# Norms of the first block: sums of squares spread by a matrix of ones, and the reciprocal root taken on full rows

## Chip, cores, metric

The kernel runs on one core of a Trainium2 chip. The metric is the device time of one execution in microseconds; lower is better. Engines are named as the profile names them: PE (TensorE), PEld (its weight loads), DVE (VectorE), ACT (ScalarE), POOL (GpSimd), SP (SyncE, which issues most DMAs here).

## The reference, cut to what matters

A first block of two transformer layers works on two streams of 256 tokens by 1024 features, `x` and `ctx`; a second block of two more layers works on `x` alone. The change touches the modulated norms of the first block, other than the very first:

```python
def _rms_norm(x, g):
    y = xf * lax.rsqrt(jnp.mean(xf * xf, axis=-1, keepdims=True) + EPS)
    return y * g
def _modulate(x, g, shift, scale):
    return _rms_norm(x, g) * (1 + scale) + shift
...
for i in range(DEPTH):
    ax = _modulate(hx, norm1_g[i], sx1, cx1)
    ac = _modulate(hc, norm1_g[i], sc1, cc1)
    ...mixer...
    hx = hx + gx1 * yx
    hx = hx + gx2 * _mlp(_modulate(hx, norm2_g[i], sx2, cx2), mlp_w1[i], mlp_w2[i])
    if with_ctx:
        hc = hc + gc1 * yc
        hc = hc + gc2 * _mlp(_modulate(hc, norm2_g[i], sc2, cc2), mlp_w1[i], mlp_w2[i])
```

## The kernel before

**Layout.** Activations are feature-major: `hx` and `hc` are eight tiles each of 128 features by 256 tokens. A weight product is made in three passes (L322 to L324): every fp32 matrix is split into a high part and a remainder (`whi`, `wlo`; `ahi`, `alo`), and PE multiplies high by high, high by low and low by high. ACT makes the high parts (L198 for weights, L369 for activations), DVE the remainders (L201, L370).

**A norm** needs, for each token, a sum over features, that is over partitions and over eight tiles. `sq_stats` squares the tiles on ACT (L736), POOL adds the first five squares into `sqa` (L741, L743), and PE multiplies the four remaining tiles, as stationary operand, by a column of ones (L748). The result is a column: one number a token, tokens in the 128 partitions, two columns for 256 tokens. `rsqrt` turns it into 1/root: DVE multiplies and adds (L330), POOL raises to the power -0.5 (L332), both on 128 partitions x 2 columns. The modulation wants that number in every partition along a row of 256 tokens, so `bcast_cols` has PE spread the columns (L725: a column repeated 128 times as moving operand's stationary, times the identity). Then, for each of the eight tiles, DVE scales by it (L757), ACT adds the shift and makes `ahi`, DVE makes `alo`.

**Five calls** of `norm` take this way. I number them in order of time:
- N1 and N2 (L1112): before the MLP of layer 0, for `hx`, then for `hc`. The residuals of `hx` (L837) come from products of the output projection; those of `hc` follow.
- N3 and N4 (L1119): before layer 1, at the end of the MLP of layer 0, again `hx`, then `hc`.
- N5 (L1399): before the MLP of layer 1, `hx` alone.

After N1, PE works on the 96 products of `hc`'s residuals, then on 96 products that need only N1 (`order="x"`), and then on products that need N2. After N3 it is 96 products for `hc`, then 96 for queries of `hx`, then keys that need both streams (512 columns wide). After N5 every product needs N5.

**Order.** Each engine executes its instructions in the order in which they stand. That order is made when the program is built, by a scheduler that works from estimated costs, not from measured ones. `Weave` interleaves attention and products by due times written in the code. Weights are fetched and split a few tiles ahead (`Weights.get`). The other norms (the first one, those of the second block) have code of their own and stay.

Of the kernel before, what the change touches and what calls it, by code (L numbers as in the profile page):

```python
# [9 lines left out]
F32 = mybir.dt.float32  # L10
F32R = mybir.dt.float32r
I32 = mybir.dt.int32
AF = mybir.ActivationFunctionType
OP = mybir.AluOpType
# [3 lines left out]
D = 1024  # L18
# [204 lines left out]
def cols(c, n=128):  # L223
    return slice(n * c, n * c + n)
# [48 lines left out]
class Net:  # L273
# [275 lines left out]
    def start(self, first):  # L549
# [76 lines left out]
        with self.tc.manual_schedule(engines={mybir.EngineType.PE}):  # L626
# [18 lines left out]
            for op in ("a00 t b a01 l m0 f0 f1 a10 a11 m1 a20 a21 m2 f2 f3 "  # L645
                       "a30 a31 m3 f4 f5 f6 f7").split():
                o, i = op[0], op[1:]
                if o == "a":
                    part(int(i[0]), int(i[1]), cell)
                elif o == "m":  # L650
                    modulate(int(i), cell["gt"])
                elif o == "f":
                    prods(int(i))
                elif o == "t":
                    for k in range(4, 8):
                        turn(1, k)
                elif o == "b":
                    nc.scalar.copy(rb, self.bcast_cols(rstd, 4, "mm"))
                elif o == "l":
                    load("a30 a31")  # L660
# [68 lines left out]
    def sq_stats(self, tiles):  # L729
# [19 lines left out]
                                 skip_group_check=True)  # L749
        return p  # L750

    def modulate(self, h, rb, gs, sh, his, los, tok):

        nc = self.nc
        for k in range(8):
            t = self.e([128, 256])
            nc.vector.scalar_tensor_tensor(t, h[k], gs[:, k:k + 1], rb, op0=OP.mult, op1=OP.mult)  # L757
            op = self.split(his[k][:, tok], los[k][:, tok], t, sh[:, k:k + 1])
            if k == 1 and tok.start == 0:
                self.W.hold = op.ins  # L760
            if k == 1 and tok.start == 0:
                self.W.ahold = self.hi_op.ins

    def norm(self, l, which, r, h, a, ss=None):

        if ss is None:
            ss = self.sq_stats(h)
        rstd = self.rsqrt(ss, 2, 1.0 / D, 1e-6, True)
        rb = self.bcast_cols(rstd, 2)
        gs, sh = self.norm_scale(l, which)  # L770
        self.modulate(h, rb, gs[:, :, r], sh[:, :, r], a[0], a[1], cols(r, 256))

# [999 lines left out]
```

## Time and profile before

| | |
|---|---|
| Median of 3 runs | 1458.98 us (1456.5 to 1461.35) |
| Profiled execution: its own time | 1455.87 us |
| Profiled execution: span | 1454.1 us |
| PE busy | 1387.4 us, 95% of the span |
| DVE, ACT, POOL busy | 72%, 44%, 20% |
| Mean granted clock of PE | 0.979 of full speed |

The profile is of one execution; the runs differ from each other by 0.3%. "Busy" counts the time in which an engine executes, the chain is the sequence of work and waits that ended last.

### The profile page before, as it was taken

What the parts mean: (1) busy time and instruction counts of PE and PEld (TensorE: products, weight loads), DVE (VectorE), ACT (ScalarE), POOL (GpSimd) and SP (SyncE); (2) the same over time, 40 slices, a digit from 0 to 9 for tenths busy, and PEclk for the clock granted to TensorE, in tenths of its full rate; (3) what the DMA queues carried; (4) which work ended last, traced back from release to release, by engine and by line L of the source; (5) the groups of instructions that cost most, each with busy time, mean ns of one, the idle gap of its engine ahead of it and who ended that gap; (6) DMA issues with size and microseconds to landing.
All of it is one profiled execution on the core that took longest, in us unless ns stands there. A gap on an engine that the chain in (4) does not pass through costs nothing.

```text
span 1454.1 us, 24709 instructions
## 1 busy us (share of the span) xinstructions
PE 1387.4 (95%) x9585; PEld 1205.9 (83%) x9585; DVE 1049.6 (72%) x1958; ACT 642.8 (44%) x1229; POOL 294.1 (20%) x281
## 2 busy tenths in 40 slices
PE   6899999999999999999999999999899998799997
PEld 4676668988778777898989989999798788698787
DVE  4587666648977788788677766666696667886756
ACT  4355435442233222245556454544454552455552
POOL 0210010231011110151000021111302347602423
PEclk9999999999999999999999989999899999999999
DMA  9826461136577897753222155655356454454452
GB/s 315 284 73 210 141 208 41 59 110 206 168 238 269 274 304 257 270 165 100 73 88 87 59 170 178 189 188 173 111 168 194 131 185 139 131 136 149 139 157 73
DMA packets 198116, 240.32 MB, mean 165 GB/s; under 512 B 21071, under 2 KB 178544, under 8 KB 198000
## 3 DMA queue, kind: packets, MB, share of 16 engines
q1 hardware_dynamic: 188912, 234.85, 50.4%
q10 hardware_dynamic: 8576, 3.89, 1.0%
q8 instruction: 75, 1.23, 0.3%
q14 instruction: 41, 0.34, 0.1%
q0 software_dynamic: 512, 0.02, 0.0%
HBM read 236.70 MB, written 2.02 MB: 164 GB/s over the span
## 4 chain that ended last, share of the span: by engine, by line
PE 77%; DVE 10%; DMA 5%; POOL 3%; issue 2%; ACT 2%; SPq 0%; DVEq 0%; ACTq 0%; POOLq 0%
PE mm L322 21%; PE mm L323 21%; PE mm L324 21%; DMA adaw<-in_ada_w 3%; DVE wlo L201 2%; PE om L1082 2%; PE pt L1066 1%; PE s L1473 1%; PE om L1490 1%; PE mm L502 1%; PE om L1333 1%; PE s L1014 1%; PE pt L1484 1%; DMA rpbs<-rpb 1%; DVE ks L1255 1%
## 5 line engine op out<-in xcount | busy, mean ns | idle before, releaser
L201 DVE TENSOR_TENSOR wlo<-raw,whi 128x1024 fp32r<-128x1024 f32 (+3 forms) x278 | 358.8, 1299 | 135.0 <-ACT whi L198 124.5
L198 ACT CAST whi<-raw 128x1024 fp32r<-128x1024 f32 (+3 forms) x282 | 288.9, 1033 | 333.6 <-PE mm L323 246.6
L322 PE MATMUL mm<-ahi,whi 128*128 128x256 f32 (+2 forms) x1232 | 397.4, 323 | 2.5 <-ACT ahi L369 2.3
L323 PE MATMUL mm<-alo,whi 128*128 128x256 f32 (+1 forms) x1232 | 394.5, 321 | 3.4 <-DVE alo L370 3.3
L324 PE MATMUL mm<-ahi,wlo 128*128 128x256 f32 (+1 forms) x1232 | 393.4, 320 | 0.0
L322 PEld LDWEIGHTS mm<-ahi,whi 128*128 128x128 f32 (+1 forms) x1232 | 236.8, 192 | 23.9 <-issue 3.2
L323 PEld LDWEIGHTS mm<-alo,whi 128*128 128x128 f32 x1232 | 236.5, 192 | 21.5 <-DVE alo L370 4.2
L324 PEld LDWEIGHTS mm<-ahi,wlo 128*128 128x128 f32 x1232 | 236.0, 192 | 18.4 <-issue 2.4
L322 PE MATMUL mm<-hid,whi 128*128 128x256 f32 (+1 forms) x544 | 179.2, 329 | 0.0
L323 PE MATMUL mm<-hid,whi 128*128 128x256 f32 (+1 forms) x544 | 178.4, 328 | 0.0
L324 PE MATMUL mm<-hid,wlo 128*128 128x256 f32 (+1 forms) x544 | 178.0, 327 | 0.0
L368 POOL TENSOR_TENSOR hid<-e,hid 128x512 fp32r<-128x512 f32 x48 | 78.3, 1632 | 416.8 <-ACT hid L367 416.8
L534 DVE SCALAR_TENSOR_TENSOR acc<-adaw,cst,acc 128x1024 f32<-128x1024 f32 x98 | 125.2, 1292 | 1.3 <-DMA adaw<-in_w_ada 1.0
L322 PEld LDWEIGHTS mm<-hid,whi 128*128 128x128 f32 x544 | 102.8, 189 | 10.6 <-ACT whi L198 0.4
L324 PEld LDWEIGHTS mm<-hid,wlo 128*128 128x128 f32 x544 | 102.8, 189 | 10.0
L323 PEld LDWEIGHTS mm<-hid,whi 128*128 128x128 f32 x544 | 102.9, 189 | 9.4
L837 DVE SCALAR_TENSOR_TENSOR hx<-mm,cst,hx 128x256 f32<-128x256 f32 x160 | 72.4, 479 | 31.7 <-PE mm L324 31.4
L322 PE MATMUL mm<-whi,ahi 128*128 128x256 f32 (+1 forms) x192 | 57.3, 299 | 0.7 <-ACT ahi L1689 0.7
L324 PE MATMUL mm<-whi,alo 128*128 128x256 f32 (+1 forms) x192 | 56.0, 292 | 1.4 <-DVE alo L1690 1.4
L1136 ACT ACTIVATE e<-mm 128x512 f32<-128x512 f32 x48 | 28.6, 596 | 63.7 <-PE mm L324 63.5
L1138 DVE SCALAR_TENSOR_TENSOR e<-mm,e 128x512 f32<-128x512 f32 x48 | 33.0, 687 | 32.9 <-ACT e L1136 32.9
L323 PE MATMUL mm<-wlo,ahi 128*128 128x256 f32 (+1 forms) x192 | 55.7, 290 | 0.0
(319 smaller groups left out, 2389.3 us busy)
## 6 DMA issues: line engine op xcount, KB each, us to landing
raw<-in_mlp_w SPq DMA_DIRECT2D x128, 512.0 KB, 4.9
adaw<-in_ada_w SPq DMA_DIRECT2D x96, 512.0 KB, 5.1
raw<-in_w_in SPq DMA_DIRECT2D x64, 512.0 KB, 3.9
adaw<-in_w_ada SPq DMA_DIRECT2D x48, 512.0 KB, 5.5
raw<-in_odd_w_in SPq DMA_DIRECT2D x24, 512.0 KB, 3.5
raw<-in_w_out SPq DMA_DIRECT2D x16, 512.0 KB, 5.1
raw<-in_even_w_in SPq DMA_DIRECT2D x12, 512.0 KB, 6.0
raw<-in_even_w_out SPq DMA_DIRECT2D x8, 512.0 KB, 3.5
```

What stands on the lines that cost most here:

```text
L198: self.nc.scalar.copy(hi[:, :m], raw)
L201: (self.nc.gpsimd if on_pool else self.nc.vector).tensor_tensor(lo[:, :m], raw, hi[:, :m].bitcast(F32), op=OP.subtract)
L322: mm(ps, w[0], x[0], start=start, stop=False, skip_group_check=skip)
L323: mm(ps, w[0], x[1], start=False, stop=False, skip_group_check=skip)
L324: mm(ps, w[1], x[0], start=False, stop=stop, skip_group_check=skip)
L368: return (lo_eng or nc.vector).tensor_tensor(lo, t, hf, op=OP.subtract)
L502: nc.tensor.matmul(ps[32 * j:32 * j + 32], self.cs1[:, k, :], raw[:, 256 * j:256 * j + 256], start=k == 0, stop=k == 7)
L534: V.scalar_tensor_tensor(acc, raw, s, acc, op0=OP.mult, op1=OP.add)
L837: self.nc.vector.scalar_tensor_tensor(h[m], ps, self.adaT[l][:, base + m, r:r + 1], h[m], op0=OP.mult, op1=OP.add)
L1082: nc.tensor.matmul(o[64 * hh:64 * hh + 64, cols(q)], self.v[ab][:, 4 - nkt + i, cols(j // 2, 64)], PTs[q][:, i, hh], start=i == 0, stop=i ...
L1136: nc.scalar.activation(r, ps, AF.Relu)
L1138: V.scalar_tensor_tensor(t, ps, 0.0, r, op0=OP.max, op1=OP.mult)
```

## The change

`norm` no longer calls `sq_stats`, `rsqrt` and `bcast_cols`; a new function `inv_rms` takes their place. The squares and POOL's sums are as before. PE now multiplies a 128x128 matrix of ones (one column, repeated) as stationary operand by the four tiles of squares as moving operand, 256 columns each: the sum lands in all 128 partitions as a row. DVE multiplies and adds on 128 partitions x 256 columns, and POOL raises 128x256 to the power -0.5. The modulation reads that tile from SBUF.

```diff
+    def inv_rms(self, tiles):
+        nc = self.nc
+        p = self.psum("om", [128, 256])
...
+        sqs.insert(0, acc)
+        for i, sq in enumerate(sqs):
+            nc.tensor.matmul(p, self.ones.to_broadcast([128, 128]), sq, start=i == 0, stop=i == len(sqs) - 1)
+        rb = self.e([128, 256])
+        nc.vector.tensor_scalar(rb, p, 1.0 / D, 1e-6, op0=OP.mult, op1=OP.add)
+        nc.gpsimd.tensor_tensor(rb, rb, self.mhalf[:, 0:1].to_broadcast([128, 256]), op=OP.pow)
+        return rb
...
-    def norm(self, l, which, r, h, a, ss=None):
-        if ss is None:
-            ss = self.sq_stats(h)
-        rstd = self.rsqrt(ss, 2, 1.0 / D, 1e-6, True)
-        rb = self.bcast_cols(rstd, 2)
+    def norm(self, l, which, r, h, a):
+        rb = self.inv_rms(h)
         gs, sh = self.norm_scale(l, which)
         self.modulate(h, rb, gs[:, :, r], sh[:, :, r], a[0], a[1], cols(r, 256))
```

Two places show how it moves instructions. Line numbers behind the new function are higher by 20 (L837 becomes L857, L757 becomes L780).

PE at N1, in the middle of the products for `hc` (`mm<-y`): before,

```order
L748 MATMUL om<-cst,e 128x1 x2
L322 MATMUL mm<-y,whi 128x256
L323 MATMUL mm<-y,whi 128x256
L324 MATMUL mm<-y,wlo 128x256
L322 MATMUL mm<-y,whi 128x256
L748 MATMUL om<-cst,e 128x1 x2
L748 MATMUL om<-cst,sqa 128x1 x2
L323 MATMUL mm<-y,whi 128x256
L324 MATMUL mm<-y,wlo 128x256
L322 MATMUL mm<-y,whi 128x256
L323 MATMUL mm<-y,whi 128x256
L725 MATMUL om<-cst,sm 128x128 x2
```

and now:

```order
L324 MATMUL mm<-y,wlo 128x256
L769 MATMUL om<-sqa,cst 128x256
L769 MATMUL om<-e,cst 128x256
L322 MATMUL mm<-y,whi 128x256
L323 MATMUL mm<-y,whi 128x256
L769 MATMUL om<-e,cst 128x256 x2
L324 MATMUL mm<-y,wlo 128x256
```

The eight small products and the two that spread have become four of 256 columns; behind them stand 94 products of `hc` and then the first that needs N1. At N3 there are 92.

DVE between N1 and N2: before, from the first residual of `hc` to the affine step of N2 (L330),

```order
L837 SCALAR_TENSOR_TENSOR hc_135<-mm,cst,hc_135 128x256 x2
L370 SCALAR_TENSOR_TENSOR alo<-e,cst,ahi 128x256
L837 SCALAR_TENSOR_TENSOR hc_135<-mm,cst,hc_135 128x256 x2
L837 SCALAR_TENSOR_TENSOR hc_136<-mm,cst,hc_136 128x256 x4
L201 TENSOR_TENSOR wlo<-raw,whi 128x1024
L330 TENSOR_SCALAR sm<-om 128x2
```

and now, to the affine step L771:

```order
L370 SCALAR_TENSOR_TENSOR alo<-e,cst,ahi 128x256 x3
L857 SCALAR_TENSOR_TENSOR hc_135<-mm,cst,hc_135 128x256 x4
L857 SCALAR_TENSOR_TENSOR hc_136<-mm,cst,hc_136 128x256 x2
L201 TENSOR_TENSOR wlo<-raw,whi 128x1024
L857 SCALAR_TENSOR_TENSOR hc_136<-mm,cst,hc_136 128x256 x2
L201 TENSOR_TENSOR wlo<-raw,whi 128x1024 x2
L771 TENSOR_SCALAR e<-om 128x256
```

In both, the residuals of `hc` stand behind the modulation of `hx` (the L757/L780 rows ahead of these), now with one more weight split among them. At N4 the two residuals of `hc` and the split that stood ahead of the modulation have moved into it, and on POOL five DMA issues (L682) stand ahead of N3's power where three stood.

## Rows read from the trace of the kernel before

**Rows 1.** The page: the chain that ended last, share of the span by engine.

```profile
PE 77%; DVE 10%; DMA 5%; POOL 3%; issue 2%; ACT 2%; SPq 0%; DVEq 0%; ACTq 0%; POOLq 0%
```

**Rows 2.** Timeline of PE (start us, us, [idle before]): first products needing N1 to N5.

```profile
270.05 0.28 PE L322 MATMUL mm<-ahi,whi 128*128 128x256 f32 x1
...
288.36 0.28 PE L322 MATMUL mm<-ahi,whi 128*128 128x256 f32 x1
...
646.24 0.28 PE L322 MATMUL mm<-ahi,whi 128*128 128x256 f32 x1
...
661.12 0.40 PE L322 MATMUL mm<-ahi,whi 128*128 128x512 f32 x1
...
842.92 0.58 PE L322 MATMUL mm<-ahi,whi 128*128 128x256 f32 x1 [1.17 <-ACT ahi L369]
```

**Rows 3.** Line L332, the power, in four windows: ns min/median/max, first and last start.

```profile
L332 POOL TENSOR_TENSOR sm<-sm,cst x1: 1022/1022/1022, 14.0 to 14.0; 128x4 f32<-128x4 f32 x1
...
L332 POOL TENSOR_TENSOR sm<-sm,cst x1: 704/704/704, 839.8 to 839.8; 128x2 f32<-128x2 f32 x1
...
L332 POOL TENSOR_TENSOR sm<-sm,cst x1: 1613/1613/1613, 276.0 to 276.0; 128x2 f32<-128x2 f32 x1
...
L332 POOL TENSOR_TENSOR sm<-sm,cst x1: 1025/1025/1025, 1236.9 to 1236.9; 128x1 f32<-128x1 f32 x1
```

**Rows 4.** Timeline of DVE beside the last two of them.

```profile
275.85 1.22 DVE L201 TENSOR_TENSOR wlo<-raw,whi 128x1024 fp32r<-128x1024 f32 x1
...
1236.74 0.74 DVE L1676 SCALAR_TENSOR_TENSOR u<-z,sm,gsr 128x512 f32<-128x512 f32 x1
```

**Rows 5.** Timeline of POOL: the first two-input multiplication of 256 columns.

```profile
62.99 0.74 POOL L847 TENSOR_TENSOR e<-e,kc 128x256 f32<-128x256 f32 x1 [6.09 <-PE om L844]
```

**Rows 6.** Timeline of PE: an fp32 product of 256 columns (two passes) among others.

```profile
62.31 0.59 PE L844 MATMUL om<-e,kc 128*128 128x256 f32 x2
...
62.97 0.39 PE L323 MATMUL mm<-alo,whi 128*128 128x512 f32 x1
63.20 0.39 PE L324 MATMUL mm<-ahi,wlo 128*128 128x512 f32 x1
```

**Rows 7.** Timeline of DVE and ACT at N1.

```profile
255.93 0.88 DVE L837 SCALAR_TENSOR_TENSOR hx<-mm,cst,hx 128x256 f32<-128x256 f32 x2 [1.73 <-PE mm L324]
...
260.96 1.27 DVE L757 SCALAR_TENSOR_TENSOR e<-hx,sm,om 128x256 f32<-128x256 f32 x3 [1.51 <-PE om L725]
...
256.50 0.81 ACT L736 ACTIVATE e<-hx 128x256 f32<-128x256 f32 x2 [1.80 <-DVE hx L837]
...
261.48 0.51 ACT L369 ACTIVATE ahi<-e,cst 128x256 fp32r<-128x256 f32 x1 [4.17 <-DVE e L757]
```

**Rows 8.** Timeline of DVE and POOL at N2.

```profile
269.23 2.44 DVE L837 SCALAR_TENSOR_TENSOR hc<-mm,cst,hc 128x256 f32<-128x256 f32 x6
...
271.64 3.35 POOL L743 TENSOR_TENSOR sqa<-sqa,e 128x256 f32<-128x256 f32 x3 [1.26 <-ACT e L736]
```

**Rows 9.** Timeline of POOL and DVE at N3 and N4.

```profile
631.31 3.16 POOL L743 TENSOR_TENSOR sqa<-sqa,e 128x256 f32<-128x256 f32 x4 [0.74 <-ACT e L736]
634.40 1.48 POOL L682 DMA_DIRECT2D row<-adag  x3
...
639.61 1.26 DVE L757 SCALAR_TENSOR_TENSOR e<-hx,sm,om 128x256 f32<-128x256 f32 x3
...
646.55 2.05 DVE L837 SCALAR_TENSOR_TENSOR hc<-mm,cst,hc 128x256 f32<-128x256 f32 x5
```

**Rows 10.** Timeline of POOL at N5.

```profile
835.49 3.14 POOL L743 TENSOR_TENSOR sqa<-sqa,e 128x256 f32<-128x256 f32 x4
```

**Rows 11.** Window of PE at N5: us, busy (x instructions), granted clock, DMA share, GB/s.

```profile
843.00:849.00 6.00, 5.94 (x26) 0.50 0.00 0
```

**Rows 12.** Timeline of PE at N1: the last four of 16 small passes; the spreading.

```profile
258.52 0.58 PE L748 MATMUL om<-cst,sqa 128*128 128x1 f32 x4
...
260.15 0.71 PE L725 MATMUL om<-cst,sm 128*128 128x128 f32 x4 [0.47 <-POOL sm L332]
```

More of the change, by code (lines that the diff above doesn't have):

```diff
@@ L750, in sq_stats @@
         return p
+    def inv_rms(self, tiles):
+        nc = self.nc
+        p = self.psum("om", [128, 256])
+        sqs, acc = [], None
+        for i, t in enumerate(tiles):
+            sq = self.e([128, 256])
+            nc.scalar.activation(sq, t, AF.Square)
+            if i >= len(tiles) - 3:
+                sqs.append(sq)
+            elif acc is None:
+                acc = self.sb.tile([128, 256], F32, name="sqa", tag="sqa", bufs=2)
+                nc.gpsimd.tensor_copy(acc, sq)
+            else:
+                nc.gpsimd.tensor_tensor(acc, acc, sq, op=OP.add)
+        sqs.insert(0, acc)
[5 more added lines that the diff above has]
+        return rb
     def modulate(self, h, rb, gs, sh, his, los, tok):
```

## The prediction

> **What bounds the kernel now.** I read the chain that ended last first: PE holds 77% of it, DVE 10%, POOL 3% [rows 1], and the table has PE busy for 95% of the span. So a change off PE matters only where PE waits for it. I then looked on PE's timeline for the first product that needs each of the five norms: 270.05, 288.36, 646.24, 661.12 and 842.92 us [rows 2]. Only the last has PE idle in front of it (1.17 us there, for `ahi`). At N1 to N4 PE has other products to do while the norm is worked out, and it comes to the dependent product later than the norm does. At N5 there is nothing else to do. So what matters is how much later than now each norm is ready, less the slack at its landmark.
>
> **The price on which all rests: the power on POOL.** Before, it works on 2 columns; now on 256. The trace has no power of 256 columns, but it has three sizes [rows 3]. With DVE quiet, 2 columns took 704 ns and 4 columns 1022 ns: (1022 - 704)/2 = 159 ns for a column, on a base of 704 - 318 = 386 ns. The call of 4 columns is the kernel's first power; that it pays for a first use I doubt, since POOL's first two-input multiplication took 0.74 us for 256 columns [rows 5], as its later ones do.
>
> The other two sizes bear it out in a rougher way. A power that runs beside a DVE instruction with two SBUF inputs seems to stand still until that one ends. Of the call with 2 columns that began at 276.02 the DVE instruction ended at 275.85 + 1.22 = 277.07 and the power at 277.63, 0.56 later; of the call with 1 column, 1236.74 + 0.74 = 1237.48 and 1237.93, 0.45 later [rows 3, 4]. One column less is 0.11 to 0.12 us less.
>
> So 256 columns are 386 + 256 x 159 ns = 41.1 us if it goes on like this. Lower bound of this reading, by the second pair: 0.70 + 254 x 0.12 = 31 us. Upper, with some waiting for DVE: 44 us. The lowest price that any row allows is that of an ordinary multiplication of the same size, 0.74 us [rows 5]. I take 41.1, because it is the one value measured undisturbed on this very operation, and call it P.
>
> The Trainium skill ("GPSIMD Engine Reference", section 3.1) would say otherwise: a two-input elementwise instruction on POOL costs about 2.6 cycles an element at 1.2 GHz, by which the power would be an estimated 0.6 us and its start, and the sum would be a gain as in the first rival below. The trace agrees for the multiplication (0.74 us) and not for the power, whose two extra columns cost 318 ns.
>
> **The other prices.** An fp32 product of 256 columns delays PE by 0.43 us: from the start of L844's pair to that of the second product behind it are 0.66 us, of which one ordinary product is 0.23 [rows 6]. Four are 1.7 us. The affine step is one DVE instruction on 128x256, like one of the three that took 1.27 us: 0.45 with its end [rows 7]. From the first modulating instruction to its `ahi` are 261.99 - 260.96 = 1.03 us [rows 7].
>
> **Norm by norm.** Each line: when the power may start, its end, the first product, and the landmark.
> - N1. The last residual ends at 256.81, its square at 257.31 [rows 7]; the last two ones products follow (0.9) and the affine step: 258.6. Power until 299.7, product at 300.8. It stands 30.7 us behind 270.05. Slack was 10.4.
> - N2. On DVE the residuals of `hc` stand behind N1's modulation, which waits for the power; ACT's squares, POOL's sums and the ones products are queued behind those. Before, from the first modulating instruction (260.96) to the last residual of `hc` (271.67) were 10.7 us, and POOL's sum ended 3.3 later [rows 7, 8]. Now one more weight split stands among them (1.2 us, as in [rows 4]). So 299.7 + 10.7 + 1.2 + 3.3 + 1.7 + 0.45 = 317.1, power until 358.2, product at 359.2 against 288.36: 70.9 us, N1's share in it. PE's 96 products between (18.3 us before) end at about 319 and wait.
> - N3. POOL's sum ends at 634.47; five DMA issues of 0.49 stand ahead of the power [rows 9]: 636.9, by which time the ones products and the affine step are done too. Power until 678.0, product at 679.1: 32.9 us.
> - N4. First modulating instruction to last residual of `hc` were 648.60 - 639.61 = 9.0 [rows 9]; two residuals and a split have moved in (0.9 + 1.2), then 3.3, 1.7 and 0.45 as at N2: 678.0 + 16.5 = 694.5. Power until 735.6, product at 736.7 against 661.12: 75.6 us, N3's share in it. The three splits ahead of the affine step fit into the wait for POOL's sum.
> - N5. The sum ends at 838.63 [rows 10]. PE has run dry; four ones products take 1.7 us at full and 3.4 at half clock, I take 2.5. Affine step 841.6, power until 882.7, product at 883.75 against 842.92: 40.8 us.
>
> Sum: 70.9 + 75.6 + 40.8 = 187.3 us. PE's clock: at N5 now, after some 7 us of little work, the granted clock was 0.50 (1.2 of 2.4 GHz) from 843 to 849 [rows 11], which loses 3 us. N2 and N4 would have such a restart anew: + 6. At N1 and N3 it costs nothing, since PE then waits for N2 and N4.
>
> What goes on PE hides in these waits: 16 small passes (four groups of 0.5), the spreading (0.71) and the wait ahead of it (0.47) [rows 12]. That DVE reads the row from SBUF and not from PSUM, and that the tile holds one of six `e` buffers during the modulation, I take as nothing: POOL waits on nobody then, and five buffers are left. The weights of the next stage are loaded during the waits, but only as far as the ring of raw tiles reaches, so little is won back.
>
> Total: 187 + 6 = 193 us, on the profiled execution's 1455.87: **1649 us**. The median of the runs is 3 us above that execution, so the median may lie there too.
>
> **Rivals.**
> 1. *The power is as cheap as a multiplication* (0.74 us): the 4-column call was slow for a reason of its own. Then N1 to N4 stay hidden, and PE saves at each 2.0 + 0.71 + 0.47 - 1.7 = 1.5 us; N5 is ready at 841.6 + 0.74 + 1.05 = 843.4, 0.5 later than now. In all -5.5: 1450 us, faster. For it: the row of 0.74 us; against it: all three sizes of the power. This decides below about 4.4 us for the power (17 ns a column): there N5 loses 4.1 and N4, whose slack ends at 3.4, another 2.
> 2. *Long rows are interleaved*, so that a column costs a quarter of 159 ns: power 10.6 us. N1 loses nothing, N2 +9.8 (299.7 becomes 269.2, then 17.4 + 10.6 + 1.0 against 288.36), N3 and N4 together +14.5, N5 +10.3, some clock: about 1494 us. For it: rows of 1, 2 and 4 columns can't show what a loop does with 256. Against it: 2 to 4 shows no saving. The Trainium skill (same page, section 7) bears on this: a chain of dependent fp32 operations pays 4 cycles for each, and four independent chains hide that; no run here shows whether the power does so.
> 3. *The row is not needed as early*: the waits at N1 and N3 are absorbed, N2 and N4 begin early since POOL's sums don't depend on them. Then each pair costs one power: 2 x (41 - 10) + 41 + 6, about 1564. Against it: DVE's order, in which `hc`'s residuals stand behind the modulation of `hx`.
>
> **Chances and range.** The forecast 0.66 (its own range, from powers of 31 and 44 us in five places, 1599 to 1664); rival 1 0.15; rival 2, with all prices between 5 and 30 us, 0.15; rival 3 0.04. 0.3% (4 us) is about what a measurement of this kernel can tell from no change. Rival 1 gives 0.10 faster, 0.05 the same; the rest is slower: 0.85. For 8 in 10 the range takes in the forecast's own and most of rivals 2 and 3: 1485 to 1675.
>
> **What would show it.** In the changed profile L772 five times with about 41 us each, and POOL's busy time up by 200 us; PE idle before the first `mm<-ahi` at N1 (some 31 us), N2 (38), N3, N4 and N5, put down to ACT's `ahi`; the clock at half behind each. If L772 takes below 5 us, the price is wrong and rival 1 or 2 holds. If it takes 41 us and the sum is off, my queues at N2 and N4 are.

## The result and the profile after

The changed kernel takes 1667.39 us (median of 4 runs, 1664.2 to 1670.23), the kernel before 1458.36 in the same comparison: ratio 1.1434, 95% interval 1.1412 to 1.1456. The profiled execution's own time is 1664.62, its span 1662.8, 208.7 us more than before.

The page, beside [rows 1]: busy time, share of the span and instructions of two engines; PE's granted clock in tenths, in 40 slices; the chain that ended last.

```profile
PE 1399.8 (84%) x9525; PEld 1213.5 (73%) x9525; DVE 1047.1 (63%) x1958; ACT 643.4 (39%) x1229; POOL 500.4 (30%) x281
...
PEclk9999997659999999976599996899999999899999
...
PE 67%; POOL 15%; DVE 10%; DMA 4%; issue 2%; ACT 2%; SPq 0%; ACTq 0%; DVEq 0%; POOLq 0%
```

PE's busy time is nearly that of before; what was added is time in which it waits. POOL is busy 206 us more and holds 15% of the chain instead of 3%. The line of the power (ns min/median/max, first and last start), against [rows 3]:

```profile
L772 POOL TENSOR_TENSOR e<-e,cst x5: 41119/41145/41148, 256.6 to 1007.6; 128x256 f32<-128x256 f32 x5
```

What PE waited for (us in total, times, longest), its two largest waits:

```profile
PE mm L322 <- ACT ahi L369: 173.3, 6, 42.9
...
PE om L769 <- POOL sqa L766: 26.7, 5, 13.2
```

PE's timeline has the five first products of [rows 2] again, each now with its idle time in brackets, and the ones products at N2 and N4:

```profile
298.87 0.58 PE L322 MATMUL mm<-ahi,whi 128*128 128x256 f32 x1 [31.73 <-ACT ahi L369]
...
313.32 1.22 PE L769 MATMUL om<-sqa,cst 128*128 128x256 f32 x2 [13.23 <-POOL sqa L766]
...
316.69 1.68 PE L769 MATMUL om<-e,cst 128*128 128x256 f32 x4
...
361.22 0.58 PE L322 MATMUL mm<-ahi,whi 128*128 128x256 f32 x1 [32.52 <-ACT ahi L369]
...
759.08 0.58 PE L322 MATMUL mm<-ahi,whi 128*128 128x256 f32 x1 [31.99 <-ACT ahi L369]
...
773.56 1.22 PE L769 MATMUL om<-sqa,cst 128*128 128x256 f32 x2 [8.83 <-POOL sqa L766]
...
820.15 0.80 PE L322 MATMUL mm<-ahi,whi 128*128 128x512 f32 x1 [33.04 <-ACT ahi L369]
...
1049.83 0.58 PE L322 MATMUL mm<-ahi,whi 128*128 128x256 f32 x1 [42.85 <-ACT ahi L369]
```

POOL's timeline has what stands between: at N2 and N4 its last adds and the power.

```profile
306.81 6.46 POOL L766 TENSOR_TENSOR sqa<-sqa,e 128x256 f32<-128x256 f32 x4
318.99 41.12 POOL L772 TENSOR_TENSOR e<-e,cst 128x256 f32<-128x256 f32 x1 [5.72 <-DVE e L771]
...
766.74 6.77 POOL L766 TENSOR_TENSOR sqa<-sqa,e 128x256 f32<-128x256 f32 x4
777.89 41.15 POOL L772 TENSOR_TENSOR e<-e,cst 128x256 f32<-128x256 f32 x1 [4.38 <-DVE e L771]
```

Cut at the ends of the last residuals of `hx` and at the first products, the two executions compare as follows (us; the last residuals of `hx` end at 256.81, 633.05 and 837.11 before, at 254.00, 712.76 and 1002.05 now):

| stretch | before | now | more by | forecast |
|---|---|---|---|---|
| start to last residual of `hx`, layer 0 | 256.81 | 254.00 | -2.8 | 0 |
| from there to N2's product (N1, N2) | 31.55 | 107.22 | 75.7 | 70.9 |
| N2's product to the last residual ahead of N3 | 344.69 | 351.54 | 6.9 | 3 |
| from there to N4's product (N3, N4) | 28.07 | 107.39 | 79.3 | 75.6 |
| N4's product to the last residual ahead of N5 | 175.99 | 181.90 | 5.9 | 3 |
| from there to N5's product | 5.81 | 47.78 | 42.0 | 40.8 |
| N5's product to the end | 611.18 | 612.97 | 1.8 | 0 |
| sum | | | 208.7 | 193 |

The first and the last stretch hold no changed norm. In the runs below they differ from before by up to 3.7 us either way, so a difference of that size between two single executions says little.

### The profile page after: what moved, and what is told of

Its sections match the earlier page's. It is cut to its first block, busy times and chain, and to the rows that moved or that the text cites. A ratio compares the mean times of both kernels' runs of the same rounds, so it can differ in the third digit from the quotient of the medians.

```text
span 1662.8 us, 24577 instructions
## 1 busy us (share of the span) xinstructions
PE 1399.8 (84%) x9525; PEld 1213.5 (73%) x9525; DVE 1047.1 (63%) x1958; ACT 643.4 (39%) x1229; POOL 500.4 (30%) x281
## 4 chain that ended last, share of the span: by engine, by line
PE 67%; POOL 15%; DVE 10%; DMA 4%; issue 2%; ACT 2%; SPq 0%; ACTq 0%; DVEq 0%; POOLq 0%
PE mm L322 18%; PE mm L323 18%; PE mm L324 18%; POOL e L772 12%; DVE wlo L201 2%; PE om L1102 2%; DMA adaw<-in_ada_w 2%; PE pt L1086 1%; PE s L1493 1%; POOL sqa L766 1%; PE om L1510 1%; PE om L769 1%; PE mm L502 1%; DVE alo L370 1%; PE om L1353 1%
## 5 line engine op out<-in xcount | busy, mean ns | idle before, releaser
L322 PE MATMUL mm<-ahi,whi 128*128 128x256 f32 (+2 forms) x1232 | 403.3, 328 | 176.6 <-ACT ahi L369 173.3
L323 PE MATMUL mm<-alo,whi 128*128 128x256 f32 (+1 forms) x1232 | 400.5, 325 | 3.6 <-DVE alo L370 3.3
L324 PE MATMUL mm<-ahi,wlo 128*128 128x256 f32 (+1 forms) x1232 | 398.6, 324 | 0.0
L322 PEld LDWEIGHTS mm<-ahi,whi 128*128 128x128 f32 (+1 forms) x1232 | 241.4, 196 | 200.5 <-ACT ahi L369 175.1
L324 PEld LDWEIGHTS mm<-ahi,wlo 128*128 128x128 f32 x1232 | 240.7, 196 | 18.8 <-issue 2.4
L772 POOL TENSOR_TENSOR e<-e,cst 128x256 f32<-128x256 f32 x5 | 205.7, 41136 | 17.3 <-DVE e L771 17.3
L369 ACT ACTIVATE ahi<-e,cst 128x256 fp32r<-128x256 f32 x64 | 28.6, 500 | 250.0 <-DVE e L780 238.9
L857 DVE SCALAR_TENSOR_TENSOR hx<-mm,cst,hx 128x256 f32<-128x256 f32 x160 | 72.2, 477 | 32.5 <-PE mm L324 32.2
L780 DVE SCALAR_TENSOR_TENSOR e<-hx,sm,e 128x256 f32<-128x256 f32 x24 | 10.3, 479 | 123.8 <-POOL e L772 123.8
L867 POOL TENSOR_TENSOR e<-e,kc 128x256 f32<-128x256 f32 x21 | 16.8, 800 | 143.6 <-PE om L864 143.6
L780 DVE SCALAR_TENSOR_TENSOR e<-hc,sm,e 128x256 f32<-128x256 f32 x16 | 6.8, 478 | 82.5 <-POOL e L772 82.5
```

What stands on the lines that cost most here:

```text
L322: mm(ps, w[0], x[0], start=start, stop=False, skip_group_check=skip)
L323: mm(ps, w[0], x[1], start=False, stop=False, skip_group_check=skip)
L324: mm(ps, w[1], x[0], start=False, stop=stop, skip_group_check=skip)
L369: self.hi_op = nc.scalar.activation(hi, t, AF.Identity, bias=sh)
L772: nc.gpsimd.tensor_tensor(rb, rb, self.mhalf[:, 0:1].to_broadcast([128, 256]), op=OP.pow)
L857: self.nc.vector.scalar_tensor_tensor(h[m], ps, self.adaT[l][:, base + m, r:r + 1], h[m], op0=OP.mult, op1=OP.add)
```

## The experiments

My theory: the power costs 41 us because it goes column by column, and each of the loss's terms is a power that stands on a path with no cover. Rivals: another part of the row form (the affine step, the wide ones products, their order on PE) costs it; or a norm's slack is met only once in a pair, so that losses don't add up.

**e1: the power becomes a multiplication** (the root is left out).

```diff
-        nc.gpsimd.tensor_tensor(rb, rb, self.mhalf[:, 0:1].to_broadcast([128, 256]), op=OP.pow)
+        nc.gpsimd.tensor_tensor(rb, rb, self.mhalf[:, 0:1].to_broadcast([128, 256]), op=OP.mult)
```

> The changed kernel with a multiplication in place of the power on POOL, same tiles and order, so the norms' values are wrong. My theory: the whole loss is the power's price for 256 columns. Then the instruction takes 0.74 us, PE's waits for ahi at the five norms are gone but for about 1 us at the last, and the time is about 1450 us (1446 to 1456). Rival: the new form itself (ones products that stand between products on PE, an affine step behind weight splits on DVE) holds a good part of the loss; then it stays above 1470 us.

Measured: 1462.06 us, ratio to the kernel before 1.0023 [1.0013, 1.0033]. The loss of 209 us is gone, so the power is its cause. The gain of 5.5 us that my first rival gave for this case isn't there, and the time lies above the 1446 to 1456 that I expected. The line of the multiplication:

```profile
L772 POOL TENSOR_TENSOR e<-e,cst x5: 610/615/615, 258.3 to 845.6; 128x256 f32<-128x256 f32 x5
```

What PE waited for most:

```profile
PE om L769 <- POOL sqa L766: 13.0, 5, 5.4
```

And PE's timeline at N2:

```profile
274.45 1.22 PE L769 MATMUL om<-sqa,cst 128*128 128x256 f32 x2 [5.43 <-POOL sqa L766]
```

The change puts the product with POOL's sum ahead of the three others (`sqs.insert(0, acc)`); before, it came last. PE takes its instructions in order and stops there for 13.0 us in all.

**e2: powers of five sizes**, one at each norm; the rest of the tile goes without a root.

```diff
-        nc.gpsimd.tensor_tensor(rb, rb, self.mhalf[:, 0:1].to_broadcast([128, 256]), op=OP.pow)
+        np_, n = {1: (128, 128), 2: (128, 32), 3: (32, 256), 4: (128, 8), 5: (128, 64)}[self.nth]
+        nc.gpsimd.tensor_tensor(rb[:np_, :n], rb[:np_, :n], half[:np_].to_broadcast([np_, n]), op=OP.pow)
```

> The changed kernel with the power on a part of the row alone, another part at each norm (N1 128 columns in 128 partitions, N2 32 in 128, N3 256 in 32 partitions, N4 8 in 128, N5 64 in 128), the rest left without it, so values are wrong. My theory, 0.386 us and 159 ns for a column however many partitions: 20.7, 5.5, 41.1, 1.7 and 10.6 us. Rival, a price by elements: N3 at a quarter, about 10.5 us. Second rival, a loop that needs many columns to get up to speed or pays by blocks: N2, N4 and N5 off that line by more than 10%.

The groups of that line (busy us, mean ns):

```profile
L775 POOL TENSOR_TENSOR e<-e,cst 32x256 f32<-32x256 f32 x1 | 41.2, 41155 | 0.3 <-DVE e L771 0.3
...
L775 POOL TENSOR_TENSOR e<-e,cst 128x128 f32<-128x128 f32 x1 | 20.7, 20747 | 2.9 <-DVE e L771 2.9
...
L775 POOL TENSOR_TENSOR e<-e,cst 128x64 f32<-128x64 f32 x1 | 10.5, 10530 | 2.7 <-DVE e L771 2.7
...
L775 POOL TENSOR_TENSOR e<-e,cst 128x32 f32<-128x32 f32 x1 | 6.3, 6328 | 5.0 <-DVE e L771 5.0
```

The fifth, 128x8, took 1669 ns. The line 386 ns + 159 ns a column, drawn from 2 and 4 columns, gives 20.74, 10.56 and 1.66 us for 128, 64 and 8 columns. A quarter of the partitions saves nothing (32x256: 41.16). Only the 32 columns take more (5.47 by the line), which alone would speak for the second rival; but DVE began a weight split 0.16 us ahead of that power, and none ran beside the four others:

```profile
298.86 1.22 DVE L201 TENSOR_TENSOR wlo<-raw,whi 128x1024 fp32r<-128x1024 f32 x1
```

The power began at 299.02, so 1.06 us of the split ran beside it, and it took 0.85 us more than the line. The whole kernel took 1537.82 us, in a single run.

**e3 and e4: the root without POOL's power**, as a bit trick with three Newton steps on DVE (e3: 11 DVE instructions in place of the affine step and the power), or as one instruction on ACT that takes scale and bias too (e4).

```diff
-        nc.vector.tensor_scalar(rb, p, 1.0 / D, 1e-6, op0=OP.mult, op1=OP.add)
-        nc.gpsimd.tensor_tensor(rb, rb, self.mhalf[:, 0:1].to_broadcast([128, 256]), op=OP.pow)
+        nc.scalar.activation(rb, p, AF.Abs_reciprocal_sqrt, scale=1.0 / D, bias=1e-6)
```

> The changed kernel with the affine step and the power replaced by an initial guess from the bits and three Newton steps on DVE (11 instructions of 128x256, some 0.4 us each, 4.6 us a norm); values right. My theory: with no power on POOL, N1 to N4 are hidden again, N5 is ready 4.6 - 0.42 - 0.74 = 3.4 us later than in the multiplication's run: about 1454 us (1448 to 1462). Rival (the form itself costs): above 1470 us. If DVE's 4 x 4.6 us at N1 to N4 are not hidden: up to 1475.

> The changed kernel with the affine step and the power replaced by one instruction on ACT (the reciprocal root of the absolute value, scale 1/1024 and bias 1e-6 within it), which reads the sum from PSUM. My theory: about 0.5 us and two loads of ACT's tables a norm, hidden at N1 to N4; 1447 to 1460 us. Rival (the form itself costs): above 1470 us.

Measured: e3 1473.53 us, ratio 1.0102 [1.0086, 1.0119]; e4 1464.63, 1.0044 [1.0027, 1.006]. In both PE again waits 13.3 and 13.6 us at the product of POOL's sum; in e3 another 11.3 for `ahi`. Both times lie above what I expected (1448 to 1462 and 1447 to 1460): I had counted only the root's own price, as in e1.

**e5 and e6: POOL's sum last**, in e1 (e5) and in e4 (e6).

```diff
-        sqs.insert(0, acc)
+        sqs.append(acc)
```

> The multiplication's run again (values wrong), with POOL's sum as the last of the four ones products in place of the first. In that run PE stood 13.0 us before the ones products, waiting for POOL's sum; my theory is that this in-order wait ate the 5.5 us that I had forecast for a cheap power. Then the wait falls by about 1.3 us at each norm (three products of 0.43 us are done meanwhile) and more at N2, whose ones products now stand 10 products further back: 4 to 9 us less than the multiplication's 1462, that is 1453 to 1458. Rival: the wait is covered by the same products anyway, or the difference of 4 us is of another origin (the start of the program); then 1460 to 1463.

> The run with ACT's reciprocal root, with POOL's sum as the last of the four ones products; values right. My theory: the same 4 to 9 us off its 1464.6, so 1456 to 1461, the same as before the change. Rival: no difference, 1463 to 1466. Faster than 1453 neither expects.

Measured: e5 1452.45 us against 1456.12, ratio 0.9973 [0.9962, 0.9985], 9.6 us below e1 (7.9 if each is taken against the kernel before beside it); so the place of one product costs that. Cut as in the table above, e1 takes 5.6 us more than before in the five stretches from the last residual ahead of N1 to N5's product, e5 0.7 less; that e5's profile is also 3.7 us shorter behind N5's product, where nothing was changed, isn't the work of the norms. e6 1454.31, 0.9991 [0.9978, 1.0004]: no difference from the kernel before, and 10.3 us below e4 (8.6 taken as above). What PE still waits for at the ones products in e5:

```profile
PE om L769 <- ACT e L759: 5.6, 5, 2.7
```

and in e6:

```profile
PE om L769 <- ACT e L759: 6.6, 3, 2.9
```

**e7 and e8: the change for `hx` alone** (N1, N3, N5), and **for `hc` alone** (N2, N4); the other norms as before.

```diff
-        rb = self.inv_rms(h)
+        if r == 0:
+            rb = self.inv_rms(h)
+        else:
+            rb = self.bcast_cols(self.rsqrt(self.sq_stats(h), 2, 1.0 / D, 1e-6, True), 2)
```

> The change at N1, N3 and N5 (hx) alone, N2 and N4 as before; values right. My theory, one power of 41.1 us on the chain of each, N1 and N3 less their slack of some 10 us, N5 in full, restarts of PE's clock besides: about 31 + 33 + 42 + 6 on 1458, 1565 us (1555 to 1580). Rival, a price that goes by the number of powers: three fifths of 209 us, 1583.

> The change at N2 and N4 (hc) alone, the other three as before; values right. My theory: N2 about 31 us past its landmark, N4 34, two restarts of 3: 1458 + 71, 1529 us (1518 to 1538). With the run for hx the two losses then add up to some 25 us less than the whole change's 209, since each pair has slack to use once. Rival, each power for itself: two fifths of 209 us, 1541, and the two add up.

Measured, in a single run each: 1589.48 and 1542.2 us, 133.4 and 86.1 above the 1456.12 of before. Together that is 219.5, not 25 less than the whole change but more (7.5 of the 11 us more lie ahead of N1 and behind N5's product). My times of 1565 and 1529 fall; the rival's, 1583 and 1541, came closer. PE in e7, the first products of N1, N3 and N5 and what it meets behind the first two, with N2's product:

```profile
301.10 0.58 PE L322 MATMUL mm<-ahi,whi 128*128 128x256 f32 x1 [31.74 <-ACT ahi L369]
...
310.49 1.01 PE L748 MATMUL om<-cst,e 128*128 128x1 f32 x4 [7.95 <-ACT e L736]
...
328.84 0.29 PE L322 MATMUL mm<-ahi,whi 128*128 128x256 f32 x1
...
723.37 0.58 PE L322 MATMUL mm<-ahi,whi 128*128 128x256 f32 x1 [30.95 <-ACT ahi L369]
...
733.65 1.01 PE L748 MATMUL om<-cst,e 128*128 128x1 f32 x4 [5.53 <-ACT e L736]
...
974.46 0.58 PE L322 MATMUL mm<-ahi,whi 128*128 128x256 f32 x1 [42.86 <-ACT ahi L369]
```

and in e8, those of N2 and N4:

```profile
325.12 0.58 PE L322 MATMUL mm<-ahi,whi 128*128 128x256 f32 x1 [34.04 <-ACT ahi L369]
...
738.17 0.79 PE L322 MATMUL mm<-ahi,whi 128*128 128x512 f32 x1 [33.88 <-ACT ahi L369]
```

Between the last residual ahead of N1 and the one ahead of N3 lie 376.24 us before, 419.02 in e7 (255.36 + 0.88 to 672.43 + 2.83), 415.82 in e8 (257.31 + 0.88 to 671.18 + 2.83) and 458.76 in the change: +42.8 and +39.6 make 82.4, of 82.5. In the second pair, up to N5's residual, +47.2 and +41.3, of 85.2. In e7, N1's product is 31.6 us late, as forecast (30.7 at N1); then PE does a few products and stands 7.95 us more, in order, at the squares of `hc`, whose residuals waited on DVE behind N1's modulation. The other 3 us or so go at half clock. In e8 the product is 35.4 us late and 4.2 follow.

That the totals add up doesn't make each power a loss for itself. N1's lateness does reach N2, as I had it: in e7, where N2 is as before, N2's product comes 72.60 us after the last residual of `hx` (328.84 - 256.24), 41.05 later than before. With e8's 35.4 that is 76.4, where the whole change has 75.7 (46.9 and 36.1, of 79.3, in the second pair). What I had wrong is that e7 would keep the slack. N1's product is late by the power less its slack, but on the way from there to N2's product PE, stopped at the squares and at half clock, takes 27.7 us where it took 18.3, and the slack is used up. So a pair's slack comes off about once, in e8 as in the whole change.

**e9: the whole change, POOL's sum last.** The edit is that of e5, with the power.

> The whole change with its power on POOL, but the product with POOL's sum stands last among the four ones products, not first. PE no longer stops at it while three other products and, at N2 and N4, the products of hx wait behind it (26.7 us of waits in the change). My theory, each power for itself: those waits only move, since PE then does the products of hx earlier and stands longer in front of the product that needs N2; won are the parts of 5.7 and 4.4 us between the sum's end and the power's start that are more than 2, so 1661 +- 2 us. Rival: the waits at the sum add to the powers, and without them the time falls by most of 26.7 us: 1642 us.

Measured, in a single run: 1653.38 us, 11.2 below the changed kernel's profiled execution and some 8 below my 1661. What PE waited for:

```profile
PE mm L322 <- ACT ahi L369: 175.9, 6, 42.8
...
PE om L769 <- ACT e L759: 13.8, 4, 6.3
```

So of the 26.7 us at the sum 16.4 moved (13.8 to the squares, 2.6 more for `ahi`), and the rival's 1642 isn't reached; but I undercounted what is won: from the last residual to the product 3.7 us at N2 (253.98 to 357.46), 3.6 at N4, and 2.7 at N5, which I had left out. These make 10.0 of the 11.2.

**e10 and e11: why PE still waits in e6.** At N2 in e6, ACT's last square waits 3.35 us for POOL, and PE 2.92 behind it. e10 gives the tile `e` eight buffers; e11 lets POOL add three squares instead of five.

```diff
-        return self.sb.tile(list(shape), dt, name="e", tag="e", bufs=6)
+        return self.sb.tile(list(shape), dt, name="e", tag="e", bufs=8)
```

```diff
-            if i >= len(tiles) - 3:
+            if i >= len(tiles) - 5:
```

> As e6 (row form, POOL's sum last, root on ACT), with 8 instead of 6 buffers of the tile e, in which the squares and the row live; the order of instructions is the same. In e6 ACT waited 3.35 us at N2 for a buffer that POOL's adds still read, and PE behind it 2.92 us, twice. Theory A, buffers: those waits go and 5 us are won: 1449. Theory B, POOL: its two last adds take 4.9 us beside DVE's weight splits, so that PE then waits for the sum in place of the square and the time stays at 1454.

> As e6, but POOL adds three squares instead of five, and PE multiplies six tiles instead of four by the ones: ten more fp32 products of 0.43 us in all. By theory B of e10 the sum is there some 3 us earlier at N2 and N4, the waits of 6.6 us in e6 go and 4.3 us of PE time come: 1452. By theory A (buffers) the same, as POOL frees them earlier. If neither holds, 1458.

Measured: e10 1454.26 us against 1457.49, ratio 0.9977 [0.9968, 0.9987], level with e6's 1454.31 though expected at 1449 by theory A; e11 1450.42, 0.9955 [0.994, 0.9969]. In e10 ACT's wait stayed (3.34 us), and PE's:

```profile
PE om L769 <- ACT e L759: 6.6, 3, 2.9
```

So the time of theory B came, without its mechanism: PE stands at the square as before. Whether more buffers than eight would end ACT's wait wasn't tried. With three adds it is gone; POOL's timeline at N2 in e10, its two last adds:

```profile
270.08 4.89 POOL L766 TENSOR_TENSOR sqa<-sqa,e 128x256 f32<-128x256 f32 x2 [0.34 <-ACT e L759]
```

In e11, its only two:

```profile
270.66 1.55 POOL L766 TENSOR_TENSOR sqa<-sqa,e 128x256 f32<-128x256 f32 x2
```

And by the groups of lines PE in e11 has 0.2 us of idle time in all before its ones products (last column):

```profile
L769 PE MATMUL om<-e,cst 128*128 128x256 f32 x50 | 12.6, 391 | 0.2
```

e11 is the fastest version that still takes the root, 0.45% below the kernel before; e10 is 0.23% below it. Both intervals exclude no change, but they are differences of 7 and 3 us.

**e12: is it the row form or the fewer adds?** The kernel before, with the edit of e11 in the sums of its five norms and the columns kept.

```diff
-            if i >= len(tiles) - 3:
+            if i >= len(tiles) - pe:
...
-            ss = self.sq_stats(h)
+            ss = self.sq_stats(h, 5)
```

> The kernel before (columns, spreading, small power) with the one edit of e11 besides the row form: in its five norms POOL adds three squares instead of five and PE multiplies six tiles instead of four by the ones, 40 more small passes. It tells whether e11 won by the row form or by the earlier sum. Theory, row form: before, PE waits only 2.5 us in all at the ones passes and 4.2 at the spreading, so that an earlier sum can win little and the passes cost 40 x 0.11 us: 1459, within 0.3% of the kernel before. Rival, earlier sum: it is N5 and the buffers that gained: 1452.

Measured: 1463.51 us, ratio 1.004 [1.0024, 1.0056]: slower than I thought, and no gain. So neither part wins alone: fewer adds on columns lose, the row form with a cheap root and five adds (e6) is level, and only both together (e11) gain. Whether ACT's root on columns, with fewer adds, would do as well wasn't tried. Most of e11's 7 us can be placed: in its profile it takes 4.3 us less than before from the last residual of `hx` to N2's product (258.07 to 285.32), 0.3 less in the second pair, 0.9 less at N5 (838.20 - 833.28 = 4.9 us against 5.8) and 0.5 less ahead of N5, 6.0 in all. That execution took 1454.2, the longest of e11's six, and spent 4.3 us more than before in the first and the last stretch.

## Why the prediction was right, and where its sizes were off

The forecast was 1649 us and a loss of 193 on the profiled execution, which lost 208.7. Its own time, 1664.62, and the median, 1667.39, lie just past the 1599 to 1664 that I gave the forecast itself, inside the wide range alone. The mechanism stood; some sizes were short. Over the forecast are 9.7 us ahead of the products of N2, N4 and N5, and 6.8 behind those of N2 and N4.

**The price of the power** held: 41.12 to 41.15 us where 41.1 was worked out from 2 and 4 columns, with POOL 206 us busier. e1 shows that the loss goes with it; e2 that neither my second rival (interleaving: nothing of it up to 256 columns) nor a surcharge on the kernel's first power is there, since the sizes from 8 to 256 columns lie on the line that the first power helped to draw. The Trainium skill ("GPSIMD Engine Reference", section 3.1), by whose 2.6 cycles an element the power would be an estimated 0.6 us, agrees with the multiplication (0.61 in e1) and not with the power.

**Five places** held too. The third rival (each pair costs one power) falls: 75.7 and 79.3 us a pair are near two, less the slack once. PE's idle time before N1 (31.7; 31 was said) and the order N1, then `hc`'s residuals, then N2 came as worked out; at N2 32.5 came where I said 38, because PE had stood 13.2 us at POOL's sum and did the products of `hx` later, under N2's power.

**Mis-sized: POOL's sum to the power's start.** The forecast had 3.3 us from the last residual of `hc` to the sum's end and 1.7 + 0.45 to the start of the power at N2 and N4. The first was 3.65 and 4.79. From the sum's end to the power it was 5.72 and 4.38, and 4.02 at N5 where 3.0 were taken: the sum's product came first and the three others after it (at N2 with products of `hx` among them), on a PE whose granted clock was 0.50 from 313.0 to 316.7 and from 773.5 to 777.4, and 0.57 at N5. In e9, with the sum last, these times are 2.32, 1.63 and 1.37, 8.8 us less.

**Mis-sized: what follows the products of N2 and N4**, 6.9 and 5.9 us instead of the 3 each that I gave a restart of the clock. Windows of PE behind N2's product (us, busy (x instructions), granted clock, DMA share, GB/s):

```profile
361.00:365.00 4.00, 3.71 (x15) 0.50 0.00 0
365.00:369.00 4.00, 1.01 (x7) 0.90 0.00 0
369.00:373.00 4.00, 4.00 (x23) 0.57 0.00 0
373.00:380.00 7.00, 7.00 (x60) 1.00 0.50 151
```

Before, the four microseconds behind the same product ran at 1.00. Now they run at 0.50 (1.2 of 2.4 GHz); then PE stops again for 2.99 us, for a small tile of DVE's (L480), and after that is at half clock anew. At half clock the products begin 0.21 us apart, at the full one 0.12. By that I estimate 2.1 us lost in the first stretch (16 products) and 1.4 in the second (15); with the wait between them these are 6.5 of the 6.9. So one restart cost less than my 3 us, and what I had left out is the second wait and the second restart. N4 has the like: 3.13 us for ACT at 825.15.

**Rival 1's time was wrong** though its condition was not met: with a cheap power the change gives 1462 (e1), not 1450. When PE doesn't stop for POOL's sum it gives 1452.45 (e5), 3.7 us below the kernel before it, of which only 0.7 lie in the norms' stretches; so the saving of 5.5 isn't shown in full by any run. In the order of instructions the sum's product stood first at N1, and I priced it without asking when its operand comes.

**Left out:** losses outside a pair's own power. In e7 a late N1 costs 11 us behind its product that I had not seen, and N1's slack is not kept at N2; in the whole change these lie inside the pair's 107 us.

## What to carry to other kernels

Before a small operation is made wide, look how its time grows with columns: two sizes in the trace of before gave this one to 0.2%, while the power on columns cost 0.7 us and the spreading behind it as much [rows 3, 12]. An operation that is cheap in total but in a chain between two matrix products costs its full length, once at each place without cover. A product that waits on the slowest engine goes last among those that it is summed with; that order alone was worth some 8 to 11 us here (e5, e6, e9).

## What the runs showed of the hardware

- The power on POOL costs 159 ns a column from 2 to 256 columns, and the same on 32 partitions as on 128. The multiplication of 256 columns took 0.61 us.
- Powers of one size differ by what DVE does: in e8 the power at N2, begun 0.16 us after a split began (the rows below), took 0.9 us longer than 41.12, the time of those with nothing on DVE beside them. Two adds of POOL took 4.89 us beside splits (e10) and 1.55 without (e11). The Trainium skill ("SBUF — State Buffer", "Who interferes with whom") has it that a DVE instruction with two inputs in SBUF contends with a POOL instruction that reads there; these rows agree. DVE's timeline in e8:

```profile
281.80 1.22 DVE L201 TENSOR_TENSOR wlo<-raw,whi 128x1024 fp32r<-128x1024 f32 x1
```

and POOL's:

```profile
281.96 42.04 POOL L772 TENSOR_TENSOR e<-e,cst 128x256 f32<-128x256 f32 x1 [4.45 <-DVE e L771]
```

- ACT makes the reciprocal root of 128x256 from PSUM in 0.38 us, with 1.28 us for a table ahead of it at three of the five norms (e6).
